# Low parts of the keys beside zeros: score products over 128 rows instead of 64

## The chip, the cores and the metric

The kernel runs on one core of one Trainium2 chip. The metric is device time in microseconds (us) of one execution. TensorE (PE) multiplies; it needs a weight load (PEld) ahead of each matmul. VectorE (DVE), ScalarE (ACT) and GpSimd (POOL) work on what comes out, and SyncE (SP) issues the DMAs of the weights.

## The reference, cut to what matters

A network of four layers over 512 tokens of 1024 channels. The parts that the change touches are the scores of two kinds of attention. In the fourth macaron layer, "stick breaking":

```
z = jnp.einsum("bqhd,bkhd->bhqk", qb, kb).astype(jnp.float32) * scale     # 16 heads of 64 channels
log_1m = jnp.where(mask, jax.nn.log_sigmoid(-z), 0.0)
between = lax.cumsum(log_1m, axis=3, reverse=True) - log_1m
att = jnp.where(mask, jnp.exp(jax.nn.log_sigmoid(z) + between), 0.0)
```

In each of the two hybrid layers after it, an attention of 8 heads over 2 groups of keys, with three branches: compressed keys (32 blocks), selected keys and windowed keys. With 512 tokens the last two branches are plain causal softmax attention over all earlier tokens. The scores of all three are products of q and k over 64 channels.

## The kernel before, in words

Everything is kept as [channels, tokens]: 128 channels on the partitions, 512 tokens along a row. To keep float32's accuracy with matmuls in the type fp32r, each operand is split into a high part (rounded to fp32r) and a low part (the rest). A dense product is then three matmuls: high by high, high by low, low by high (`three`, L274).

For the scores the heads have only 64 channels, so the three products fit into two matmuls. `query` (L1008) puts the high part of a head's q above (or below) its low part in one tile of 128 rows. `key` (L1020) makes a tile for each of the two heads of a pair in which the head's high part stands twice, above and below, and a third tile `low` with the low parts of both heads, one in each half. In `stick` (L1124) the first product runs over all 128 rows: q's high and low part against k's high part. The second multiplies k's low part by q's high part, and since these stand in one half of the partitions only (`hs`), it runs over 64 rows. The third matmul of each group adds the mask: a bf16 identity against a bf16 table with -1e30. A head has four such groups, for key tiles 0 to 3, with 512, 384, 256 and 128 queries.

The hybrid layers do the same with `doubled` (L1654), which makes the tiles of high parts and of low parts for both groups of heads, and `products` (L1648), a first matmul over 128 rows and a second over 64. `scores` (L1671) calls it for each of 4 heads of a group and adds a mask; the query tile i is the stationary operand and (i + 1) * 128 keys move. `blocks` (L1721) calls it for the 32 compressed keys, without a mask.

So there are 64 groups in `mixer1` (16 heads by 4), and in each hybrid layer 64 with a mask (8 steps by 2 groups by 4 heads) and 32 of the compressed keys: 192 with a mask, a quarter of them of each width, and 64 without.

In `mixer1` (L1002) the work of the heads overlaps. While the scores of a head are made, DVE and ACT turn those of the head before into weights, and the projections of later heads (`more`, L1075) fill in on TensorE. The last two heads have no such filler. In `nsa` (L1662) eight steps go through the same pattern: scores of one group, values of the step before, scores of the other group; `cnt` (L1765) says how far gating and retention go on at each point. A scheduler orders the instructions of each engine from this. Each engine then runs its own in that order, and waits on semaphores.

Tiles of 128x512 come from one pool of `A_BUFS` buffers (L24); PSUM has 8.

```
self.mm(z[i], k[h][:, at], q[h][:, i * P:], i != 3, False, True)          # L1135
self.mm(z[i], k[2][hs, at], q[h][hs, i * P:], False, False, True)         # L1136
self.mm(z[i][:, :P], self.masks[:, :P], self.masks[:, P:2 * P], False, True, True)
```

Of the kernel before, what the change touches and what calls it, by code (L numbers as in the profile page):

```python
# [15 lines left out]
P = 128  # L16
# [7 lines left out]
A_BUFS = 70  # L24
# [31 lines left out]
def rwkv_tables():  # L56
    """Masks for one chunk of 64 tokens, the same on both halves of the partitions: strict, identity, a level's block
    with odd rows and even columns (l = 1, .., 32), the first one transposed, the scan's restart; then the causal
    mask of two chunks side by side."""
# [44 lines left out]
class Net:  # L104
# [56 lines left out]
    def load_consts(self):  # L161
        self.consts = self.pool.tile([P, CONST.shape[1]], F32, name="consts")
        self.nc.sync.dma_start(self.consts, self.t["consts"])
        # masks that the tensor engine adds to scores: identity, and -1e30 where a key isn't before its query
        # [keys, queries] or comes after it [queries, keys]
# [51 lines left out]
    def weave(self, *gens):  # L217
        """The steps of several generators, each given with their number, in proportion."""
        todo = [[0.0, i, 1.0 / n, x] for i, (x, n) in enumerate(gens)]
        while todo:  # L220
            at = min(todo)
            at[0] += at[2]
            if next(at[3], self) is self:
                todo.remove(at)

# [1 line left out]
    def wsplit(self, w, k0, nk, segs, rows=None, pairs=False):  # L227
        """Columns segs of rows of k tiles k0.. of w, as high and low parts."""
# [15 lines left out]
        if pairs:  # L244
            # columns (g, r, d) come to stand as (r, g, d)
# [16 lines left out]
    def chunks(self, w, segs, kt, kc=4, rows=None, pairs=False, start=0):  # L262
        """For one chunk of k tiles after another: indices and (high, low) parts, 128 columns each."""
# [15 lines left out]
    def gemm(self, w, segs, rhs, kc=4, begun=None, **kw):  # L279
        """[columns, tokens], one PSUM tile for 128 columns of each of segs; begun: what begin() returned."""  # L280
# [8 lines left out]
    def begin(self, w, segs, rhs, out, kc=4, **kw):  # L289
        """The first len(rhs) of gemm's k tiles, in steps."""  # L290
# [8 lines left out]
    def by_halves(self, w, segs, rhs, **kw):  # L299
        """The same, but for one half of the tokens after the other, each in PSUM tiles of its own."""  # L300
# [9 lines left out]
    def opening(self, start, rhs):  # L310
        """A layer's first products: loads its weights, then goes over the first and the second half of the tokens."""
# [13 lines left out]
    def gemm_tok(self, w, segs, rhs):  # L325
        """[tokens of j, columns segs of w], one PSUM tile for each j."""
# [20 lines left out]
    def tok_pair(self, ws, rhs, jj):  # L347
        """[tokens of 2 jj and of 2 jj + 1, 256 columns], side by side; pauses half way."""
# [13 lines left out]
    def column_tile(self, w, c0, rhs, every=4):  # L362
        """[128 columns, tokens]; pauses after so many k tiles."""
# [8 lines left out]
    def token_sums(self, accs, ps):  # L372
        """Means over the channels, tokens on partitions: one column of PSUM for 128 tokens of each."""
# [19 lines left out]
    def spread(self, r, ps):  # L393
        """[128, n] with tokens on partitions -> PSUM [128, 128 n], the same on all partitions."""
# [80 lines left out]
    def postnorm(self, w, rhs, gname, feed, start, rows=None, begun=()):  # L475
        """x + rmsnorm(w^T rhs), and the next layer's operands and first products."""
# [47 lines left out]
    def hidden(self, w, rhs, psl, evacuate, between=None):  # L524
        """A layer's pairs of gate and up tiles; those of one step are taken up after the next step's products."""
# [33 lines left out]
    def head_rsqrt(self, sqs, ones, value, op):  # L559
        """The power -1/2 of the heads' sums of sqs, on all of a head's channels: a PSUM tile for each."""  # L560
# [26 lines left out]
    def mixer0(self, rhs, psl, feed, start):  # L587
# [16 lines left out]
        # halves for sigmoid(x) = tanh(x / 2) / 2 + 1 / 2  # L604
# [15 lines left out]
        def shift(n, ps):  # L620
            """Column tile n of the projection, mixed with its predecessor in time."""
# [17 lines left out]
        # the products of these four come before the statistics of x  # L639
# [25 lines left out]
        def quadrants(ps, lhs, rhs_):  # L665
            """A product for each chunk of each head."""
            for n in range(8):
                for rows in both:
                    self.mm(ps[rows, n * 64:n * 64 + 64], lhs(rows, n), rhs_(rows, n))
# [9 lines left out]
        def prepare(p):  # L679
            """Operands of two heads, [(head, channel), tokens]."""  # L680
# [36 lines left out]
        def pair(p):  # L717
            """Two heads up to the scan; [(chunk's parity, token), (head, chunk / 2, 64)]."""
# [23 lines left out]
            # what isn't on the way to the inverse goes on beside it  # L742
# [73 lines left out]
        def scan(p):  # L816
            """Two heads over the chunks."""
# [35 lines left out]
        def norm(p):  # L853
            """The normalisation of what a scan gave, and the gate."""
# [45 lines left out]
        # streams side by side, each with the weight of its steps  # L900
# [11 lines left out]
    def rglru(self, w_in, rhs, R, yb):  # L912
# [29 lines left out]
        def recurrence(p):  # L942
# [11 lines left out]
            # y = 8 r softplus, a = exp(-y), sqrt(1 - a^2) = sqrt(tanh(y) (1 + a^2))  # L954
# [24 lines left out]
    def softplus_neg(self, lam, scale):  # L979
        """scale * log(1 + exp(-lam)) on [128, 4], to float32's accuracy."""  # L980
# [21 lines left out]
    def mixer1(self, rhs, psl, feed, start):  # L1002
# [5 lines left out]
        def query(ps, scale):  # L1008
            """High and low parts of each head's channels above each other."""
# [10 lines left out]
        def key(ps):  # L1020
            """High parts of each head's channels, twice; low parts."""
# [3 lines left out]
            a, b, low = self.A(F32R), self.A(F32R), self.A(F32R)  # L1025
            nc.scalar.copy(a, o)
            self.tt(low, o, a.bitcast(F32), SUB)
# [3 lines left out]
            return a, b, low  # L1031
# [8 lines left out]
        def products(b, jj):  # L1040
            """Values of four heads, two token tiles side by side."""
# [82 lines left out]
    def stick(self, q, k, h, masks):  # L1124
        """One head's weights; columns of the scores of key tile i: queries from tile i on."""
# [4 lines left out]
        hs = slice(h * 64, h * 64 + 64)  # L1130
# [771 lines left out]
```

## Time and profile before

| | |
|---|---|
| median of 3 runs | 3677.62 us (3674.2 to 3680.09) |
| span of the profiled execution | 3671.4 us |
| TensorE busy | 98% of the span, 20664 matmuls |
| weight loads | 80% |
| VectorE / ScalarE / GpSimd busy | 58% / 37% / 3% |
| mean granted TensorE clock | 0.979 |

The profiled execution has its own time, and the page and all rows are of it: its span is 6.2 us below the median of the runs. TensorE counts as busy while a matmul is recorded as under way, which includes time in which it waits for its weights. So a busy share of 98% does not mean that nothing can be saved there; the distance from the start of one matmul to the start of the next tells more. In a timeline a row "x2" holds two matmuls that follow each other, under the shape of the first.

### The profile page before, as it was taken

To read this page: it belongs to the slowest core of one execution; us is meant where nothing else is said; L and a number is where in the kernel's file an instruction comes from. 1 tells how busy PE (TensorE), PEld (TensorE's weight loads), DVE (VectorE), ACT (ScalarE), POOL (GpSimd) and SP (SyncE) were. 2 spreads that over 40 slices of the span, in tenths; PEclk is the share of its full clock that TensorE was granted. 3 is DMA by queue.
4 is the path that set the end of the run, shared out by engine and by line. 5 is a ranking of instruction groups with operands and counts; after the bars stand their busy time and mean duration, and the time that the engine had idled before them with its cause. 6 is when DMAs were issued, how large, how long until landed. Compare 5 with 4: busy or idle time off the path is not lost.

```text
span 3671.4 us, 50427 instructions
## 1 busy us (share of the span) xinstructions
PE 3603.1 (98%) x20664; PEld 2926.5 (80%) x20664; DVE 2113.8 (58%) x3463; ACT 1357.6 (37%) x2220; POOL 125.8 (3%) x156
## 2 busy tenths in 40 slices
PE   8999999999999999999999999999999999999998
PEld 7888777788888888977888888657888886588887
DVE  5442777565436764576576646546654465466645
ACT  3332433133223222376432224433543354344432
POOL 0000001000000000000000001001000020010000
PEclk9999999999999999999999999989999999899999
DMA  4222310022324554311166533101323331013321
GB/s 139 94 94 89 98 42 18 26 87 95 96 88 134 192 189 135 95 52 52 58 196 189 171 114 82 41 18 46 102 94 97 112 90 35 12 47 109 98 92 63
DMA packets 359896, 337.85 MB, mean 92 GB/s; under 512 B 20214, under 2 KB 341040, under 8 KB 359664
## 3 DMA queue, kind: packets, MB, share of 16 engines
q1 hardware_dynamic: 358624, 332.46, 29.2%
q8 instruction: 162, 2.65, 0.3%
q0 software_dynamic: 1040, 2.16, 0.2%
q14 instruction: 70, 0.57, 0.1%
HBM read 332.48 MB, written 2.10 MB: 91 GB/s over the span
## 4 chain that ended last, share of the span: by engine, by line
PE 94%; DVE 3%; issue 1%; ACT 1%; POOL 1%; DMA 1%; SPq 0%; POOLq 0%; DVEq 0%; ACTq 0%
PE p L152 92%; DVE a L140 1%; PE p L1714 1%; DMA wr<-in_l_ffn_w_in 0%; POOL s L384 0%; ACT a L137 0%; DVE a L143 0%; PE p L1195 0%; ACT wh L252 0%; PE p L583 0%; DVE wl L140 0%; PE p L660 0%; DMA a<-in_x 0%; ACT a L1716 0%; POOL a L1305 0%
## 5 line engine op out<-in xcount | busy, mean ns | idle before, releaser
L152 PE MATMUL p<-a,wh 128*128 128x512 f32 (+1 forms) x8920 | 2538.9, 370 | 16.4 <-ACT a L137 6.9
L152 PEld LDWEIGHTS p<-a,wh 128*128 128x128 f32 x8920 | 1613.4, 190 | 315.0 <-issue 23.6
L152 PE MATMUL p<-a,wl 128*128 128x512 f32 (+1 forms) x4460 | 1634.3, 367 | 0.0
L140 DVE TENSOR_TENSOR wl<-wr,wh 128x1024 fp32r<-128x1024 f32 (+2 forms) x561 | 639.4, 1142 | 792.4 <-ACT wh L252 784.9
L152 PEld LDWEIGHTS p<-a,wl 128*128 128x128 f32 x4460 | 845.9, 190 | 138.7 <-issue 3.4
L252 ACT CAST wh<-wr 128x1024 fp32r<-128x1024 f32 (+2 forms) x545 | 541.5, 995 | 1060.4 <-PE p L152 1002.4
L152 PE MATMUL p<-a,a 64*64 64x64 f32 (+10 forms) x4360 | 486.4, 285 | 9.6 <-ACT a L1716 3.4
L140 DVE TENSOR_TENSOR a<-a,a 128x512 f32<-128x512 f32 (+6 forms) x752 | 443.7, 604 | 88.6 <-ACT a L156 59.0
L152 PEld LDWEIGHTS p<-a,a 64*64 64x64 f32 (+3 forms) x4360 | 300.3, 150 | 142.9 <-issue 81.6
L137 ACT ACTIVATE a<-a 128x512 f32<-128x512 f32 (+1 forms) x356 | 199.0, 590 | 350.1 <-DVE a L140 230.3
L140 DVE TENSOR_TENSOR a<-p,a 128x512 f32<-128x512 f32 (+5 forms) x334 | 203.6, 622 | 102.5 <-PE p L152 85.9
L156 ACT CAST a<-a 128x512 fp32r<-128x512 f32 x148 | 91.3, 619 | 265.5 <-DVE a L140 263.6
L143 DVE SCALAR_TENSOR_TENSOR acc<-wr,s,acc 128x1024 f32<-128x1024 f32 x84 | 107.7, 1283 | 79.6 <-DMA wr<-in_w_ada 79.2
L143 DVE SCALAR_TENSOR_TENSOR a<-p,cols,a 128x511 f32<-128x511 f32 (+1 forms) x176 | 125.5, 744 | 47.8 <-ACT a L137 46.3
L140 DVE TENSOR_TENSOR a<-a,p 128x256 f32<-128x256 f32 (+1 forms) x280 | 122.7, 466 | 36.0 <-PE p L152 34.7
L152 PE MATMUL p<-wh,a 128*128 128x256 f32 (+1 forms) x640 | 125.3, 292 | 0.1
L137 ACT ACTIVATE a<-a,cols 128x256 fp32r<-128x256 f32 (+3 forms) x156 | 83.3, 554 | 65.8 <-DVE a L140 65.8
L152 PEld LDWEIGHTS p<-wh,a 128*128 128x128 f32 x640 | 103.9, 195 | 4.6 <-issue 4.0
L137 ACT ACTIVATE a<-p 128x512 f32<-128x512 f32 (+2 forms) x144 | 75.7, 548 | 82.0 <-PE p L152 76.9
L152 PE MATMUL p<-wl,a 128*128 128x256 f32 (+1 forms) x320 | 92.8, 290 | 0.0
L137 ACT ACTIVATE a<-p,cols 128x512 f32<-128x512 f32 x92 | 68.8, 771 | 63.2 <-PE p L152 63.1
L1688 DVE TENSOR_REDUCE s<-p 128x1 f32<-128x512 f32 (+3 forms) x88 | 54.8, 638 | 60.1 <-PE p L152 59.7
(186 smaller groups left out, 1667.5 us busy)
## 6 DMA issues: line engine op xcount, KB each, us to landing
wr<-in_l_ffn_w_in SPq DMA_DIRECT2D x176, 512.0 KB
wr<-in_w_ada SPq DMA_DIRECT2D x96, 512.0 KB
wr<-in_w_up SPq DMA_DIRECT2D x88, 512.0 KB
wr<-in_l_ffn_w_out SPq DMA_DIRECT2D x68, 512.0 KB
wr<-in_w_in SPq DMA_DIRECT2D x40, 512.0 KB
wr<-in_w_down SPq DMA_DIRECT2D x34, 512.0 KB
wr<-in_l_w_qkv SPq DMA_DIRECT2D x24, 512.0 KB
wr<-in_l_w_in SPq DMA_DIRECT2D x22, 512.0 KB
```

The lines of the kernel that those rows point to most:

```text
L137: self.nc.scalar.activation(out, in_, func, bias=bias, scale=scale)
L140: self.nc.vector.tensor_tensor(out, a, b, op=op)
L143: self.nc.vector.scalar_tensor_tensor(out, a, s, b, op0=op0, op1=op1)
L152: self.nc.tensor.matmul(out, lhsT, rhs, start=start, stop=stop, skip_group_check=skip)
L156: self.nc.scalar.copy(hi, src)
L252: self.nc.scalar.copy(hi[:, :m], raw[:, :m])
L1688: nc.vector.tensor_reduce(nm[:, r0:r0 + per], ps[:, :per * n].rearrange("p (r n) -> p r n", r=per), axis=X, op=MAX, negate=True)
L1714: nc.tensor.transpose(ps[:, q4[r]], probs[g][r][:, q4[kt]], self.const("ident"))
```

## The change

The low parts of k get a tile for each head (or group) instead of one for both. In each such tile the head's low part stands in its half, and the other half is set to zero by GpSimd. The second product then runs over all 128 rows of the tile of q: the half that holds q's low part meets zeros. Its result is the same. Where VectorE took the low parts of a pair in one instruction of 128x512 in `key`, it now takes them in two of 64x512. The pool has one buffer more. Comments and docstrings were taken out as well, and are left out here.

```
-A_BUFS = 70
+A_BUFS = 71
 ...
         def key(ps):
             o = self.A()
             self.tt(o, ps, R, MUL)
             yield
-            a, b, low = self.A(F32R), self.A(F32R), self.A(F32R)
+            a, b, l0, l1 = (self.A(F32R) for _ in range(4))
+            nc.gpsimd.memset(l0[lower].bitcast(F32), 0.0)
+            nc.gpsimd.memset(l1[upper].bitcast(F32), 0.0)
             nc.scalar.copy(a, o)
-            self.tt(low, o, a.bitcast(F32), SUB)
+            self.tt(l0[upper], o[upper], a.bitcast(F32)[upper], SUB)
+            self.tt(l1[lower], o[lower], a.bitcast(F32)[lower], SUB)
             nc.scalar.copy(b[lower], a[lower])
             nc.vector.tensor_copy(b[upper], a[lower])
             nc.scalar.copy(a[lower], a[upper])
-            return a, b, low
+            return a, b, l0, l1
 ...
     def stick(self, q, k, h, masks):
-        hs = slice(h * 64, h * 64 + 64)
 ...
-            self.mm(z[i], k[2][hs, at], q[h][hs, i * P:], False, False, True)
+            self.mm(z[i], k[2 + h][:, at], q[h][:, i * P:], False, False, True)
 ...
     def products(self, out, q, kk, g, at, keys, start, stop):
-        gs = slice(g * 64, g * 64 + 64)
         self.mm(out, q[:, at], kk[g][:, keys], start, False, True)
-        self.mm(out, q[gs, at], kk[2][gs, keys], False, stop, True)
+        self.mm(out, q[:, at], kk[2 + g][:, keys], False, stop, True)

-    def doubled(self, ps, first, second, low):
+    def doubled(self, ps, *parts):
         halves = [slice(0, 64), slice(64, 128)]
-        for g, hi in enumerate((first, second)):
+        for g in range(2):
+            hi, low = parts[g], parts[2 + g]
+            self.nc.gpsimd.memset(low[halves[1 - g]].bitcast(F32), 0.0)
             for half in (halves[g], halves[1 - g]):
                 self.nc.scalar.copy(hi[half], ps[halves[g]])
             self.tt(low[halves[g]], ps[halves[g]], hi.bitcast(F32)[halves[g]], SUB)
```

In `hybrid` the tiles that go to `doubled` become four instead of three (`kc`, L1352; `keys`, L1382).

Around the scores the order on TensorE stays as it was: the same matmuls follow each other, and the second of a group reads other rows. What moves stands on VectorE and GpSimd. On VectorE, in `key` of the third pair of heads: the low parts (a_13032 before; a_13040 and a_13041 after) between those of the query and the copy of the high part.

```order
L140 TENSOR_TENSOR a_13025<-a_12939,a_13025 64x512
L140 TENSOR_TENSOR a_13024<-a_12939,a_13024 64x512
L140 TENSOR_TENSOR a_13032<-a_12972,a_13030 128x512
L1029 COPY a_13031<-a_13030 64x512
L1143 TENSOR_SCALAR a_13083<-p_13039 128x512
```

After:

```order
L140 TENSOR_TENSOR a_13033<-a_12947,a_13033 64x512
L140 TENSOR_TENSOR a_13032<-a_12947,a_13032 64x512
L140 TENSOR_TENSOR a_13040<-a_12980,a_13038 64x512
L140 TENSOR_TENSOR a_13041<-a_12980,a_13038 64x512
L1032 COPY a_13039<-a_13038 64x512
L1145 TENSOR_SCALAR a_13095<-p_13051 128x512
```

One subtraction has become two, ahead of the copy and of the next head's first step.

On GpSimd, in the first hybrid layer, from the zeros for the compressed values (a_18953 before, a_18988 after) on; the AFFINE_SELECT and what follows it belong to the gating part.

```order
L1635 MEMSET a_18953 128x512
L1444 AFFINE_SELECT a_19054<-a_19054 128x512
L1460 TENSOR_TENSOR s_19059<-s_19058,consts 128x4
L1460 TENSOR_TENSOR s_19245<-s_19244,consts 128x4
L1460 TENSOR_TENSOR s_19272<-s_19271,consts 128x4
```

After:

```order
L1606 TENSOR_TENSOR a_18624<-a_18598,cols_405 128x512
L1660 MEMSET a_18756 64x512
L1660 MEMSET a_18757 64x512
L1637 MEMSET a_18988 128x512
L1660 MEMSET a_18602 64x32 x2
L1660 MEMSET a_19079 64x512
L1660 MEMSET a_19080 64x512
L1446 AFFINE_SELECT a_19094<-a_19094 128x512
L1462 TENSOR_TENSOR s_19099<-s_19098,consts 128x4
```

All the new zeros of this layer stand ahead of the AFFINE_SELECT, which is the first instruction there to wait for long. In `mixer1`, where GpSimd had nothing to do, 16 such instructions stand one after the other.

## Rows read from the trace of the kernel before

**Rows 1.** The page: engines; the chain that ended last, by engine.

```profile
PE 3603.1 (98%) x20664; PEld 2926.5 (80%) x20664; DVE 2113.8 (58%) x3463; ACT 1357.6 (37%) x2220; POOL 125.8 (3%) x156
...
PE 94%; DVE 3%; issue 1%; ACT 1%; POOL 1%; DMA 1%; SPq 0%; POOLq 0%; DVEq 0%; ACTq 0%
```

**Rows 2.** Busy time of engines in the mixer, then both hybrid layers' attention; columns first.

```profile
core 0: us, PE busy (x) PEld busy (x) DVE busy (x) ACT busy (x) POOL busy (x), PEclk, DMA share, GB/s
1565.00:1765.00 200.00, 197.89 (x1073) 150.14 (x1071) 144.19 (x267) 133.67 (x266) 0.00 (x0) 0.97 0.15 45
2265.00:2490.00 225.00, 221.70 (x1122) 146.53 (x1120) 116.55 (x270) 91.88 (x238) 7.79 (x6) 0.91 0.12 34
3005.00:3220.00 215.00, 211.29 (x1064) 139.48 (x1063) 114.44 (x270) 87.13 (x230) 7.85 (x6) 0.91 0.11 30
```

**Rows 3.** Timeline of TensorE, a dense stream and two heads' scores: start, length, instructions.

```profile
1566.67 0.62 PE L152 MATMUL p<-a,wh 128*128 128x512 f32 x2
...
1567.35 0.62 PE L152 MATMUL p<-a,wh 128*128 128x512 f32 x2
...
1569.38 0.56 PE L152 MATMUL p<-a,a 128*128 128x128 f32 x2
...
1569.91 0.68 PE L152 MATMUL p<-a,a 128*128 128x256 f32 x2
...
1570.55 0.91 PE L152 MATMUL p<-a,a 128*128 128x512 f32 x2
...
1571.43 0.79 PE L152 MATMUL p<-a,a 128*128 128x384 f32 x2
...
1572.19 0.56 PE L152 MATMUL p<-a,a 128*128 128x128 f32 x2
...
1574.21 0.23 PE L152 MATMUL p<-masks 128*128 128x128 bf16 x1
1574.25 0.70 PE L152 MATMUL p<-a,wh 128*128 128x512 f32 x2
1574.79 0.40 PE L152 MATMUL p<-a,wl 128*128 128x512 f32 x1
```

**Rows 4.** Timeline of the weight loads, the group of 512 queries above.

```profile
1570.52 0.20 PEld L152 LDWEIGHTS p<-a,a 128*128 128x128 f32 x1
1570.96 0.18 PEld L152 LDWEIGHTS p<-a,a 64*128 64x128 f32 x1 [0.24 <-issue]
1571.39 0.10 PEld L152 LDWEIGHTS <-masks 128*128 128x128 bf16 x1 [0.25 <-issue]
```

**Rows 5.** Timeline of TensorE: matmuls of 256 columns; transposes of 128 columns.

```profile
1593.52 0.40 PE L152 MATMUL p<-wh,a 128*128 128x256 f32 x2
...
1593.88 0.40 PE L152 MATMUL p<-wh,a 128*128 128x256 f32 x2
...
2384.72 1.03 PE L1714 MATMUL p<-consts,a 128*128 128x128 f32 x8
```

**Rows 6.** Timeline of TensorE: one run of the compressed keys; a slow group of 384.

```profile
2340.05 3.47 PE L152 MATMUL p<-a,a 128*128 128x32 f32 x16
2343.45 0.58 PE L152 MATMUL p<-wh,a 128*128 128x256 f32 x1
...
2404.10 1.28 PE L152 MATMUL p<-a,a 128*128 128x384 f32 x2
```

**Rows 7.** What TensorE waited for in the mixer, then in the first hybrid layer.

```profile
PE p L152 <- ACT a L1030: 1.8, 1, 1.8
...
PE p L152 <- ACT a L1716: 1.7, 4, 1.0
```

**Rows 8.** Timelines of VectorE (last `key`) and of GpSimd (first hybrid layer).

```profile
1740.83 0.69 DVE L140 TENSOR_TENSOR a<-a,a 128x512 fp32r<-128x512 f32 x1
...
2213.27 0.52 POOL L1635 MEMSET a<- 128x512 f32 x1
2284.07 0.64 POOL L1444 TENSOR_SCALAR_AFFINE_SELECT a<-a 128x512 f32<-128x512 f32 x1 [70.28 <-ACT a L1442]
```

More of the change, by code (lines that the diff above doesn't have):

```diff
@@ L1351, in hybrid @@
         kcs = self.A(F32R)
-        kc = [kcs[:, i * 32:i * 32 + 32] for i in range(3)]
+        kc = [kcs[:, i * 32:i * 32 + 32] for i in range(4)]
         nc.gpsimd.dma_start(w2[0:64, 0:64], t["c_w2_k"][l])
@@ L1381, in keys @@
                 pass
-            kk.append([self.A(F32R) for _ in range(3)])
+            kk.append([self.A(F32R) for _ in range(4)])
             self.doubled(ps, *kk[-1])
```

## The prediction

> **What bounds the kernel now.** I read the page first: TensorE is busy for 98% of the span and makes up 94% of the chain that ended last [rows 1]. So a saving on TensorE counts, and one elsewhere counts only where TensorE waits for it. Then I asked for busy times in the three stretches in which the changed matmuls stand, the second mixer and the attention of the two hybrid layers [rows 2]. There too TensorE is busy for 198 of 200, 222 of 225 and 211 of 215 us, with VectorE at 72%, 52% and 53% and ScalarE at 67%, 41% and 41%. The two weight columns tell more: the loads take 150 of 200, 147 of 225 and 139 of 215 us there, against 80% of the whole span. TensorE is "busy" in these stretches partly with something that is neither streaming columns nor loading weights early. The granted clock is lower there as well, 0.97, 0.91 and 0.91, where it is 0.979 on average over the kernel.
>
> The timeline shows what that is. In the dense stream three matmuls of 512 columns take 0.68 us from start to start, 0.227 each, each with its own weight load under the one before [rows 3]. A group of scores with 512 queries has two such matmuls and a mask of 128 columns, and takes 0.88 (from 1570.55 to 1571.43); the other widths take 0.76 for 384, 0.64 for 256 and 0.53 for 128 [rows 3]. The weight loads say why: those of the 64-row product (1570.96) and of the mask after it (1571.39) start only when the matmul before has run out, after the load engine was idle for 0.24 and 0.25 us, though nothing that the profile shows held it ("issue"). The load of the next 128-row product starts at once behind the mask (1570.52, before the matmul at 1570.55) [rows 4]. So a step from 128 rows to 64 or back costs an unhidden load and the run-out of the matmul before; between two operations of 128 rows, even of different types, neither is seen.
>
> The Trainium skill has both sides of this. "TensorEngine Tiling (Array Packing)", section Key Properties, states that changing the tiling mode, not just the tile, drains TensorE; by that rule the second product brings two drains into each group and the change removes them, which rows 4 bear out with 0.24 and 0.25 us of idle loads. "TensorE: Matmul & The Clock Gate", Part 3, The mechanism, states that a weight load overlaps with a running matmul only when the row groups differ; by that rule two products of 128 rows would not overlap either, and the change would bring nothing. The dense stream of rows 3 speaks against it here, with 0.227 us for a matmul with a load of its own; it stands below as a rival.
>
> **The change part by part.** *The 192 groups with a mask.* After the change all three operations run over 128 rows. For the products I take stream prices: 0.227 for 512 [rows 3]; 0.120 for 256, from three in 0.36 [rows 5]; midway, 0.174, for 384. For 128 columns the load sets the pace: eight transposes take 1.03 us with the run-out of the last [rows 5], so under 0.129 each, and I take 0.115. The mask, and the load behind it that has only the short mask to hide under, I price where a dense stream follows: mask and two products of 512 from 1574.21 to 1574.79, 0.58, less 2 x 0.227, is 0.13 [rows 3]. New group: 0.58, 0.48, 0.37 and 0.36. Saved: 0.30, 0.28, 0.27 and 0.17, together 1.02 us for one of each width. With 48 of each width that is 49 us.
>
> *The load of the mask behind a 128-row product* is not in this trace, since every mask now follows a 64-row product. From below it costs nothing more than the 0.13 above; from above it stays unhidden as now, about 0.10 us (the mask's load, 0.10, in rows 4), 192 times: 19 us. I take the lower end, because the load behind the mask crosses the same change of type and is early [rows 4].
>
> *The 64 groups of compressed keys.* Sixteen products of 32 columns, eight pairs, take 3.40 us (2340.05 to 2343.45) [rows 6]: 0.425 a pair. At 0.115 each a pair takes 0.23; saved 0.195, times 64 is 12.5 us. Gross: 61 us, about 17 in the mixer and 22 in each hybrid layer.
>
> *The clock.* 0.03 of 200, 0.09 of 225 and 0.09 of 215 us, doubled since the low level is 0.5 (1.2 GHz, against 2.4), make some 91 us at the low level in the three stretches [rows 2]. A group of 384 that took 0.79 with its run-out at the high level takes 1.28 at the low one [rows 3, 6]: 38% of it is the clock, so 91 us hold up to 35 us to be won. The clock fell at 2343.1, right at the end of the run of compressed keys of rows 6, in which TensorE streams few columns. That run shrinks from 3.4 to 1.8 us, but transposes and short matmuls of the values stay beside it. Bounds: 0 (it falls as often as before; it could also fall more, below) and 35 us. I take 14, somewhat under half.
>
> *What is added.* VectorE: eight more subtractions in `key`. The one of 128 rows takes 0.69 us [rows 8]; one of 64 rows has the same columns, so I take 0.69, bounds 0.35 and 0.69: 5.5 us, hidden in the 28% of the mixer in which VectorE is idle, but for one place. In the last `key` TensorE already waits 1.8 us for the last copy L1030 [rows 7], which comes behind that subtraction: 0.7 us more. GpSimd: 16 zero fills of 64x512 in the mixer, 8 more and 4 of 64x32 in the hybrid layers. One of 128x512 takes 0.52 [rows 8]; GpSimd is idle in the mixer and 97% idle in the others [rows 2]. In the hybrid layers the new ones stand behind the fill at 2213.27 and ahead of an instruction that waited 70 us, until 2284.07 [rows 8], so there is room for some 2.6 us of fills. Cost nothing; if that cover were gone, at most 0.5 for each pair. No DMA is added, and SP's queue keeps its order. The buffer more takes no time.
>
> *What is late next.* When scores finish earlier, what depends on them or fills in beside them is needed earlier. In the mixer the 1.8 us of rows 7 are almost all of TensorE's waiting, in a hybrid layer 1.7 us at four places. Each of the 16 steps of the hybrid layers begins with four groups that get 0.7 to 1.2 us shorter, and the values behind them need weights that ACT and DVE make meanwhile. I take half a microsecond lost at each step: 8 us; bounds 0 and half of the gross saving, 30.
>
> Sum: 61 + 14 - 0.7 - 8 = 66 us. The profiled execution would go from 3671.4 to 3605; it stands 6.2 us below the median of the runs, and I carry that over: 3677.6 - 66 = 3612 us.
>
> **The rivals.**
> 1. The clock comes back nearly whole. For it: the fall right behind the run of compressed keys, and denser streams after the change. Against: short matmuls and transposes remain in the same places. 61 + 32 - 7 = 86 us, 3592.
> 2. The mask's load stays unhidden. For it: today it always is [rows 4]. Against: the change of rows explains that, and the way out of the mask is early. 66 - 19 = 47 us, 3631.
> 3. ACT and DVE become the bound: with 72% and 67% of the mixer they have little room once it is a tenth shorter, and the last heads have no filler. Half the gross saving is lost and the clock gains nothing: 61 - 31 = 30 us, 3648. Against: TensorE hardly waits in these stretches now [rows 7].
> 4. Nothing is saved, since full-height products with the same row groups don't overlap their loads either: 3678. Against: the stream of rows 3.
> 5. Slower: TensorE gets ahead of its operands in the attention of the hybrid layers, and in the gaps the clock falls. The gross 61 us stand against it; at 38% of a low-clock stretch lost [rows 3, 6], it decides from 160 us more at the low level than the 91 of now. With 190 more, 0.38 x 190 = 72 us are lost, net 11: 3689. For it: the clock is already lowest there. Against: TensorE would have to be slow for over half of the stretches, where today it idles 1.7 us for ACT in one of them.
>
> **How the numbers follow.** Chances: forecast 0.50, rival 1 0.20, rival 2 0.12, rival 3 0.12, rival 4 0.03, rival 5 0.03. The likeliest is 3612. The range goes from 3582, rival 1 with the whole 35 us and no step lost (61 + 35 = 96), to 3645, almost rival 3; what is outside is half of rival 3, rivals 4 and 5, and the edges. A difference under 0.2%, 7.4 us, can't be told from none here: faster by more than that 0.94, within it 0.03, slower 0.03.
>
> **What the profile after would show.** Right: no weight load of 64 rows in the scores; the load of the second product and that of the mask start just behind the start of the matmul before, and a group with 512 queries takes about 0.58 us, one with 128 about 0.36, a run of 16 products of 32 columns about 1.8. The mixer's stretch shrinks by some 17 us and each hybrid layer's by 20 to 30, with PEclk there above 0.91. Wrong: groups at 0.68 with an idle gap only ahead of the mask (rival 2), unchanged groups (rival 4), short groups with idle time of TensorE behind them that ends at ACT or DVE (rival 3), or a lower PEclk in the two hybrid stretches (rival 5). A wait for POOL in front of a product of scores would show that I hid the fills too easily.

## The result and the profile after

The changed kernel takes 3587.02 us (median of 4 runs, 3585.56 to 3588.3), beside 3675.91 us for the kernel before (4 runs, 3668.94 to 3680.09). The ratio is 0.9758, 95% interval 0.9744 to 0.9772: 89 us saved. The forecast was 66 us and 3612 us, with a range from 3582 to 3645; the nearest case is rival 1, the clock that comes back nearly whole, at 3592.

The page of the changed kernel, engines and the chain that ended last. TensorE has as many instructions as in [rows 1] and is as "busy" in share, but for 97 us less.

```profile
PE 3505.7 (98%) x20664; PEld 2884.3 (80%) x20664; DVE 2117.7 (59%) x3471; ACT 1358.2 (38%) x2220; POOL 139.3 (4%) x184
...
PE 91%; DVE 4%; issue 2%; ACT 1%; POOL 1%; DMA 1%; SPq 0%; POOLq 0%; DVEq 0%; ACTq 0%
```

The same three stretches as in [rows 2], now cut exactly at the matmuls that begin and end them in the kernel before (columns as there):

```profile
1564.50:1749.40 184.90, 177.41 (x1072) 144.31 (x1071) 148.47 (x274) 134.21 (x266) 5.21 (x10) 0.99 0.16 49
2250.40:2440.10 189.70, 184.45 (x1122) 128.60 (x1121) 115.31 (x270) 91.41 (x239) 7.86 (x6) 0.99 0.14 40
2954.40:3135.00 180.60, 175.04 (x1063) 121.65 (x1061) 113.48 (x270) 86.53 (x230) 7.86 (x6) 1.00 0.13 36
```

Between the same matmuls the mixer's stretch is 15.1 us shorter and those of the hybrid layers 35.4 and 34.2: 84.7 of the 87.5 us by which the span shrank (3671.4 to 3583.9). The granted clock, 0.97, 0.91 and 0.91 before, is 0.99, 0.99 and 1.00. Where each group of scores got shorter the timeline of TensorE shows (start, length, instructions, and in brackets a wait and what ended it). Read the distance from one start to the next.

```profile
1569.14 0.71 PE L152 MATMUL p<-a,a 128*128 128x512 f32 x2
1569.70 0.23 PE L152 MATMUL p<-masks 128*128 128x128 bf16 x1
1569.73 0.60 PE L152 MATMUL p<-a,a 128*128 128x384 f32 x2
...
1570.21 0.42 PE L152 MATMUL p<-a,a 128*128 128x128 f32 x2
...
1570.51 0.48 PE L152 MATMUL p<-a,a 128*128 128x256 f32 x2
...
1570.87 0.71 PE L152 MATMUL p<-a,a 128*128 128x512 f32 x2
...
1573.83 0.73 PE L152 MATMUL p<-a,wh 128*128 128x512 f32 x2 [2.17 <-DVE a L143]
```

A group of 512 queries takes 0.59 us (1569.14 to 1569.73), 384 takes 0.48, 128 takes 0.30, 256 takes 0.36; in [rows 3] they took 0.88, 0.76, 0.53 and 0.64. The weight loads beside them, in which the new thing is the row "x2" (both products now have 128 rows, and the second load follows the first without a gap):

```profile
1569.11 0.31 PEld L152 LDWEIGHTS p<-a,a 128*128 128x128 f32 x2
1569.69 0.10 PEld L152 LDWEIGHTS <-masks 128*128 128x128 bf16 x1 [0.27 <-issue]
1569.70 0.31 PEld L152 LDWEIGHTS p<-a,a 128*128 128x128 f32 x2
```

The two fp32r loads take 0.31 together and are over at 1569.42, while the first product is still under way. Of the two late loads of [rows 4] one is gone. The mask's load is still late (0.27 us idle, 0.25 before), so half of the prediction's sign for rival 2 is there, and the change of rows can't be the whole reason for that idle time. But it costs almost nothing: the next load starts 0.01 later, and the group already takes no more than the forecast gave it.

The run of compressed keys and the 384-query groups of the first hybrid layer, to be held against [rows 6]:

```profile
2318.80 1.86 PE L152 MATMUL p<-a,a 128*128 128x32 f32 x16
2320.50 0.37 PE L152 MATMUL p<-wh,a 128*128 128x256 f32 x1
...
2366.57 3.99 PE L152 MATMUL p<-a,a 128*128 128x32 f32 x22
...
2370.44 0.60 PE L152 MATMUL p<-a,a 128*128 128x384 f32 x2
2370.88 0.23 PE L152 MATMUL p<-masks 128*128 128x128 bf16 x1
2370.92 0.60 PE L152 MATMUL p<-a,a 128*128 128x384 f32 x2
```

Sixteen products take 1.70 us (2318.80 to 2320.50) instead of 3.40, 0.21 a pair (median of all 64 pairs 0.223). The row "x22" is a mixed one: 4 and 12 products of 32 columns, between them 4 of the values with 512 columns, and 2 of the first group of 384. A group of 384 behind such a run takes 0.48 from start to start; before it took 1.26 there, at the low clock (the 1.28 of [rows 6] is its length with the run-out).

What TensorE waited for, in the mixer and then in the first hybrid layer (us in total, times, longest):

```profile
PE p L152 <- ACT a L1033: 2.5, 1, 2.5
PE p L152 <- DVE a L143: 2.2, 1, 2.2
PE p L152 <- ACT a L1157: 1.4, 1, 1.4
...
PE p L152 <- ACT a L1719: 1.7, 4, 1.0
PE p L1717 <- ACT a L137: 1.5, 4, 1.0
```

L1033 is the last copy of `key`, L1030 in [rows 7]: 1.8 us there, 2.5 now. The wait of 2.2 us for DVE at the mixer's start is new, and that for L1157 was 0.2 (as L1155). In the hybrid layers the old 1.7 (L1716) stands as L1719, and the wait for ACT L137 grew from 0.2 to 1.5.

### The profile page after: what moved, and what is told of

Its sections match the earlier page's. It is cut to its first block, busy times and chain, and to the rows that moved or that the text cites. A ratio compares the mean times of both kernels' runs of the same rounds, so it can differ in the third digit from the quotient of the medians.

```text
span 3583.9 us, 50496 instructions
## 1 busy us (share of the span) xinstructions
PE 3505.7 (98%) x20664; PEld 2884.3 (80%) x20664; DVE 2117.7 (59%) x3471; ACT 1358.2 (38%) x2220; POOL 139.3 (4%) x184
## 4 chain that ended last, share of the span: by engine, by line
PE 91%; DVE 4%; issue 2%; ACT 1%; POOL 1%; DMA 1%; SPq 0%; POOLq 0%; DVEq 0%; ACTq 0%
PE p L152 90%; DVE a L140 2%; PE p L1717 1%; ACT a L137 1%; DVE a L143 1%; DVE wl L140 0%; POOL s L384 0%; ACT wh L252 0%; PE p L1197 0%; DMA wr<-in_l_ffn_w_in 0%; DMA a<-in_x 0%; PE p L660 0%; PE p L583 0%; DVE a L149 0%; ACT a L1719 0%
## 5 line engine op out<-in xcount | busy, mean ns | idle before, releaser
L140 DVE TENSOR_TENSOR a<-a,a 128x512 f32<-128x512 f32 (+8 forms) x760 | 449.9, 606 | 89.6 <-ACT a L156 59.0
L152 PE MATMUL p<-a,a 64*64 64x64 f32 (+9 forms) x4360 | 408.4, 275 | 14.5 <-ACT a L1719 3.4
L152 PEld LDWEIGHTS p<-a,a 64*64 64x64 f32 (+3 forms) x4360 | 269.9, 149 | 108.1 <-issue 49.2
L137 ACT ACTIVATE a<-a 128x512 f32<-128x512 f32 (+1 forms) x356 | 199.4, 591 | 343.5 <-DVE a L140 224.4
L143 DVE SCALAR_TENSOR_TENSOR acc<-wr,s,acc 128x1024 f32<-128x1024 f32 x84 | 107.8, 1283 | 84.2 <-DMA wr<-in_w_ada 84.1
L143 DVE SCALAR_TENSOR_TENSOR a<-p,cols,a 128x511 f32<-128x511 f32 (+1 forms) x176 | 125.6, 745 | 47.7 <-ACT a L137 46.2
L137 ACT ACTIVATE a<-a,cols 128x256 fp32r<-128x256 f32 (+3 forms) x156 | 83.6, 557 | 64.7 <-DVE a L140 64.7
L137 ACT ACTIVATE a<-p 128x512 f32<-128x512 f32 (+2 forms) x144 | 75.2, 548 | 75.7 <-PE p L152 70.9
L137 ACT ACTIVATE a<-p,cols 128x512 f32<-128x512 f32 x92 | 68.8, 772 | 63.1 <-PE p L152 63.0
L384 POOL TENSOR_TENSOR s<-s,consts 128x2 f32<-128x2 f32 (+1 forms) x18 | 14.5, 805 | 1674.1 <-DVE s L147 1651.5
```

The costliest lines, as they stand in the source:

```text
L137: self.nc.scalar.activation(out, in_, func, bias=bias, scale=scale)
L140: self.nc.vector.tensor_tensor(out, a, b, op=op)
L143: self.nc.vector.scalar_tensor_tensor(out, a, s, b, op0=op0, op1=op1)
L152: self.nc.tensor.matmul(out, lhsT, rhs, start=start, stop=stop, skip_group_check=skip)
L384: self.nc.gpsimd.tensor_tensor(r, v, self.const("mhalf")[:, :v.shape[1]], op=ALU.pow)
```

## The experiments

Each kernel is the changed one with the edit shown, but for one that starts from the kernel before. Times are compared with the kernel before, run beside them on the same chip.

**1. Rows of the second product back to 64, all else as changed.**

```
-            self.mm(z[i], k[2 + h][:, at], q[h][:, i * P:], False, False, True)
+            self.mm(z[i], k[2 + h][hs, at], q[h][hs, i * P:], False, False, True)
 ...
-        self.mm(out, q[:, at], kk[2 + g][:, keys], False, stop, True)
+        self.mm(out, q[gs, at], kk[2 + g][gs, keys], False, stop, True)
```

(`hs` and `gs` are the half with the head's or group's rows, as in the kernel before.)

> The changed kernel with both second products back on 64 rows (stick and the hybrid layers), while the tiles for each head, their zeros, the eight further subtractions and the 71st buffer stay. Theory 'fills cost nothing': 3674 to 3680 us, ratio to before 0.998 to 1.003, row groups as long as before (0.88 us for 512 queries). Rival 'the new tiles or the other placement of buffers are part of the gain or of a hidden loss': outside of that by more than 0.3%.

Measured: 3672.5 us, ratio 0.9997 [0.9986, 1.0007]. Tiles, fills, subtractions and the extra buffer cost nothing that can be measured over the whole kernel, and the whole gain comes from the rows of the product. By stages it is less even: between the same matmuls the mixer is 4.7 us longer than before and the second hybrid layer 6.5 shorter. The granted clock goes the same way: 0.95 in both, where it was 0.97 and 0.91 before. But the mixer has also 2.5 us of wait for L1033 and 1.6 for L1158 (L1157 in the changed kernel), with groups as long as before. So these two waits come from what was added on the other engines and not from the shorter groups.

**2 and 3. The mixer alone, the hybrid layers alone.** Only the second, then only the first half of the edit above.

> The changed kernel with the hybrid layers' second products back on 64 rows, so that only the 64 groups of the second mixer run over 128 rows. Theory 'unhidden loads at each change of row count': 17 us of groups and about 5 us of clock (the 13.7 us at the low level around 1750 go) less 2 to 5 us of waits: 3655 to 3662. Rival 'the gain is the clock's in the hybrid layers': 3670 or more.

> The changed kernel with stick's second products back on 64 rows, so that only the hybrid layers' 192 groups run over 128 rows. Theory: 44 us of groups and 20 to 28 us of clock less some 9 us of waits: 3605 to 3622, and with the mixer alone the two gains add up to that of the whole change (about 89 us) within 6 us. Rival 'the stages are linked, the mixer's clock carries over': the two don't add up.

Measured: 3652.0 us, ratio 0.9943 [0.9929, 0.9956], for the mixer; 3606.87, ratio 0.9817 [0.9805, 0.983], for the hybrid layers. In ratios 0.57% and 1.83% make 2.40%, against 2.42% for the whole change: the parts add up. The mixer's time is 3 us under the range that was expected for it.

**4. Before, with the products of 64 rows put together.** If what is saved is the step from 128 rows to 64 and back, it can also be saved without zeros: a head's (or step's) four second products stand one behind another.

```
             self.mm(z[i], k[h][:, at], q[h][:, i * P:], i != 3, False, True)
-            self.mm(z[i], k[2][hs, at], q[h][hs, i * P:], False, False, True)
-            self.mm(z[i][:, :P], self.masks[:, :P], self.masks[:, P:2 * P], False, True, True)
+            self.mm(z[i][:, :P], self.masks[:, :P], self.masks[:, P:2 * P], False, False, True)
+        for i in (1, 3, 2, 0):
+            at = slice(i * P, (i + 1) * P)
+            self.mm(z[i], k[2][hs, at], q[h][hs, i * P:], False, True, True)
```

(and the same in `scores` and `blocks`)

> The kernel before, all second products still over 64 rows from the shared tile, but those of a head (or of a group in a score step, or of a group of compressed keys) follow each other behind the 128-row products and masks. So a head or step has 2 changes of row count instead of 8. Theory A 'the cost sits at the change of row count': three quarters of the 61 us of groups and much of the clock go: 46 + 15 to 20 less waits, 3610 to 3628; 64-row loads within a run are early and the four products of 512, 384, 256 and 128 take about 0.65 us from start to start of the first to the last. Rival B 'a product over 64 rows is slow in itself, its load is never hidden': no gain, 3670 to 3685, since each of the four still shows an idle load engine ahead of it.

Measured: 3609.48 us, ratio 0.9824 [0.9811, 0.9836]: 64 us of the 89, just more than theory A's range allows, with every second product still on 64 rows. Its weight loads, then its timeline of TensorE ("x5" holds the four products of 64 rows, 384, 128, 256 and 512 columns, and the first of the next head):

```profile
1571.82 0.10 PEld L152 LDWEIGHTS <-masks 128*128 128x128 bf16 x1
1571.98 0.58 PEld L152 LDWEIGHTS p<-a,a 64*128 64x128 f32 x4
1572.82 0.19 PEld L152 LDWEIGHTS p<-a,a 128*128 128x128 f32 x1 [0.25 <-issue]
```

```profile
1571.99 1.27 PE L152 MATMUL p<-a,a 64*128 64x384 f32 x5
1573.11 0.23 PE L152 MATMUL p<-masks 128*128 128x128 bf16 x1
```

Four loads of 64 rows take 0.58 us together, without a gap, beside products that run; only the load that follows them, of 128 rows again, waits 0.25. So a product of 64 rows is not slow, a change of rows is. The step back to 128 rows agrees with what "TensorEngine Tiling (Array Packing)", section Key Properties, in the Trainium skill says: changing the mode, not the tile, drains TensorE. There are no zeros in this kernel, and its granted clock in the three stretches is 0.97, 0.98 and 0.96, so most of the clock's return doesn't depend on zeros. The rule of the Trainium skill in "TensorE: Matmul & The Clock Gate", Part 3, The mechanism, that a load overlaps a running matmul only where the row groups differ, is not borne out: here four loads into the same half follow each other, and in the changed kernel both products use all rows.

**5 and 6. Which part holds the clock.** One kernel has only the compressed keys on 128 rows, the other everything except the compressed keys:

```
-    def products(self, out, q, kk, g, at, keys, start, stop):
+    def products(self, out, q, kk, g, at, keys, start, stop, rows=None):
-        self.mm(out, q[:, at], kk[2 + g][:, keys], False, stop, True)
+        rs = rows or slice(0, P)
+        self.mm(out, q[rs, at], kk[2 + g][rs, keys], False, stop, True)
```

with `group[g]` as `rows` in `scores` (and `stick` on 64 rows) for the one, in `blocks` for the other.

> The changed kernel with all second products back on 64 rows, in the second mixer and in the hybrid layers' steps, but for the 64 groups of compressed keys, which run over 128 rows. Direct gain: 64 x 0.20 us = 13 us. Theory 'each run of compressed keys brings the clock down behind it': the low-level time in the hybrid layers falls from some 60 us to under 25, worth up to 15 us more: 3645 to 3655. Rival 'the clock falls for what stands around the runs': 13 us and no more, 3659 to 3663, with the low stretches where they were.

> The changed kernel with only the 64 groups of compressed keys back on 64 rows. Direct loss against the changed kernel's 3587: 13 us, 3600. Theory 'each run of compressed keys brings the clock down behind it': low-level time of 40 us or more comes back in the hybrid layers, 3608 to 3618, and PEclk there falls to about 0.93. Rival 'the clock falls for what stands around the runs': 3598 to 3602, with low-level time in the hybrid layers under 20 us as in the changed kernel.

Measured: compressed keys alone 3653.54, ratio 0.9945 [0.9927, 0.9964]; all but them 3621.61, ratio 0.9867 [0.9849, 0.9885]. The second is 34 us slower than the changed kernel's 3587, or 37 to 40 by the ratios, which allow for the other chip; the 64 pairs themselves take 64 x (0.424 - 0.223) = 13 us more. Its two hybrid stretches, then one piece of the first (columns as in [rows 2]), and TensorE's timeline there:

```profile
2254.40:2461.40 207.00, 202.42 (x1122) 141.21 (x1121) 115.69 (x270) 91.21 (x240) 7.85 (x6) 0.92 0.13 36
2975.20:3172.40 197.20, 191.98 (x1063) 133.85 (x1062) 114.00 (x271) 86.33 (x230) 7.85 (x6) 0.93 0.11 33
...
2378.00:2391.50 13.50, 12.83 (x44) 7.36 (x44) 6.85 (x25) 4.63 (x14) 0.00 (x0) 0.50 0.00 0
```

```profile
2374.45 6.12 PE L152 MATMUL p<-a,a 128*128 128x32 f32 x22
...
2380.45 0.99 PE L152 MATMUL p<-a,a 128*128 128x384 f32 x2
2381.24 0.33 PE L152 MATMUL p<-masks 128*128 128x128 bf16 x1
2381.33 0.99 PE L152 MATMUL p<-a,a 128*128 128x384 f32 x2
```

At 2378.0, among the same 22 matmuls that take 3.99 us in the changed kernel (2366.57), the clock falls to 0.50 (1.2 GHz, the low level), and the groups of 384 behind it, on 128 rows, take 0.88 us (2380.45 to 2381.33) instead of 0.48. In the kernel before a fall stands at that run too (the run is at 2395.8 to 2402.8 there); in the changed kernel there is none. The stretch of that fall before, then the 10 us behind the run in the changed kernel:

```profile
2394.30:2414.80 20.50, 19.82 (x65) 11.96 (x65) 8.46 (x28) 5.63 (x20) 0.00 (x0) 0.50 0.00 0
...
2370.00:2380.00 10.00, 9.32 (x52) 5.53 (x51) 6.79 (x24) 5.18 (x14) 0.00 (x0) 1.00 0.00 0
```

The two layers have eight such runs of compressed keys. In the profile of the kernel before a fall to 0.50 begins inside or less than 4 us beside all eight, in the kernel with only the compressed keys back on 64 rows at seven, with only them on 128 rows at two, and in the changed kernel at none. So the compressed keys do bring falls. They are not all of it: the kernel that changes nothing but them has the clock at 0.98 in the first hybrid stretch, as expected, but at 0.93 in the second, where its longest fall (17 us, from 3181.5) begins over 9 us from the nearest run:

```profile
2272.50:2480.40 207.90, 203.56 (x1121) 134.10 (x1120) 116.28 (x270) 91.98 (x239) 7.85 (x6) 0.98 0.13 36
2997.20:3202.90 205.70, 201.82 (x1063) 132.19 (x1063) 114.46 (x270) 86.90 (x230) 7.86 (x6) 0.93 0.11 31
```

Both parts together bring it back nearly whole. My theory, that the compressed keys alone decide, holds for one layer and fails for the other, each read from one profiled execution.

**7. The changed kernel again,** without an edit.

> The changed kernel as it is, so that the next ones stand beside it on one chip: 3585 to 3590 us, ratio to before 0.974 to 0.978.

Measured: 3588.02 us, ratio 0.9766 [0.9752, 0.9781].

**8 and 9. Going further.** High and low part of the compressed keys as one product of 64 columns, added on VectorE; then also the second of `key`'s subtractions on GpSimd, against the new wait for DVE L143.

```
-                    self.products(ps[:, r * 32:r * 32 + 32], q[r][g], kc, g, q4[i], slice(0, 32), True, True)
+                    self.mm(ps[:, r * 64:r * 64 + 64], q[r][g][:, q4[i]], kc[4][:, g * 64:g * 64 + 64])
 ...
-            self.tt(l1[lower], o[lower], a.bitcast(F32)[lower], SUB)
+            nc.gpsimd.tensor_tensor(l1[lower], o[lower], a.bitcast(F32)[lower], op=SUB)
```

> The changed kernel with the two products of each group of compressed keys made one: high and low parts of the keys stand side by side, 64 columns move past the same queries, and VectorE adds the two sums (16 more additions of 128x128, some 0.3 us each, beside other work). Theory 'a product of 32 columns is priced by its weight load': 64 x 0.11 = 7 us less, 3578 to 3583. Rival 'it is priced by its columns or by the additions behind it': 3585 to 3592.

> As the one with compressed keys of 64 columns, and the second of the two subtractions in key goes to GpSimd, so that VectorE has as many as before. Theory 'the subtraction added on VectorE is what made the wait of 2.2 us at the mixer's start and lengthened that for the last key from 1.8 to 2.5 us': 1 to 4 us less than the one before it, 3575 to 3581, and the wait for the last key back at 1.8 or below. Rival 'GpSimd is slower, and its order puts the next zeros behind the wait': a wait for POOL of 0.5 us or more in front of score products, and no gain.

Measured: 3585.39, ratio 0.9757 [0.9743, 0.9772], and 3582.41, ratio 0.9752 [0.9737, 0.9766]. The first theory's price was right: a group of compressed keys takes 0.112 us instead of 0.223 (medians), 7 us for all 64. The total fell by only 2.6 us, outside the range that the theory gave, and the intervals overlap; where the rest went stays open. The last time is the lowest of all, but its interval overlaps that of the changed kernel's second run (0.9752 to 0.9781) too, so it isn't shown to be better. TensorE's waits in its mixer say why so little came of it:

```profile
PE p L152 <- ACT a L1157: 3.6, 2, 2.1
PE p L152 <- ACT a L1033: 3.1, 2, 2.9
```

The 2.2 us for DVE L143 are gone, and the two for ACT grew from 3.9 to 6.7. The wait for the last key did not go back to 1.8, it grew to 2.9, so this theory failed. The subtraction takes 1.64 us on GpSimd (mean of 8), and VectorE's own, which runs beside it, takes 1.75 to 1.83 instead of 0.69.

**10 to 12. The mask's late load, and a miss.** Masks in fp32r, to rid the mask of its change of type:

```
-        self.masks = self.pool.tile([P, 3 * P], mybir.dt.bfloat16, name="masks")
-        self.nc.gpsimd.memset(self.masks, 0.0)
+        m32 = self.A()[:, :3 * P]
+        self.nc.gpsimd.memset(m32, 0.0)
 ...
+        self.masks = self.pool.tile([P, 3 * P], F32R, name="masks")
+        self.nc.vector.tensor_copy(self.masks, m32)
```

> The changed kernel with the masks in fp32r instead of bf16, so that no operation of a group changes the type. In the changed kernel the load of a bf16 mask still starts only when the product before it has streamed out (0.27 us idle after 512 columns). Theory 'that is the change of type': the mask's load starts early, and groups go to 0.565 us for 512 queries (-0.03), but to 0.32 for 128 (+0.02), since three loads of fp32r set the pace there; together within 3 us of the changed kernel, 3584 to 3590. Rival 'it is something of the mask itself': the load stays late, and as it is longer for fp32r, each group gets some 0.06 us longer: 12 us, 3595 to 3602.

Measured: 3642.63 us, ratio 0.9913 [0.9896, 0.993]. No forecast of the time held, but the theory's mechanism did. The load of a mask in fp32r starts early, 0.23 us ahead of its matmul (1599.12 and 1599.35) where a bf16 mask's starts 0.01 ahead (1569.69 and 1569.70 above):

```profile
1599.12 0.19 PEld L152 LDWEIGHTS p<-masks 128*128 128x128 f32 x1
...
1599.35 0.22 PE L152 MATMUL p<-masks 128*128 128x128 f32 x1
```

So it is the mask's type that keeps its load late, and an early load brings almost nothing: 512, 384 and 256 queries gained 0.01 to 0.02 us a group (512: 0.580 in the median, from 0.592), and 128 lost 0.04. What made the kernel slower stands far from the change: the dense stream went from 0.227 to 0.233 us for a matmul of 512 columns. The edit had moved all tiles in memory, since the first of them is now asked for ahead of the masks. Two more runs separate type from place: bf16 masks with the tiles at those places (the same edit, with `tile([P, 6 * P], mybir.dt.bfloat16)` for the masks), and the changed kernel with all tiles moved by 32 bytes (`3 * P + 16` for the masks' size).

> The masks stay in the short type, as in the changed kernel, but are first built in a 128x512 tile, and their tile is padded to the size that it has in the run with fp32r masks, so that all working tiles lie where they lay in that run: their first at byte 20256 instead of 23136 of a partition, the weight tiles' at 169312 instead of 168544. Nothing else differs from the changed kernel. Theory (what slowed the dense stream from 0.227 to 0.233 us for a matmul of 512 columns is where the tiles lie, not the masks' type): the stream takes 0.233 again, the groups take what they take in the changed kernel (0.59 for 512 queries), and the time is 3640 to 3655 us, ratio about 0.992. Rival (it is the masks' type, or something that the run with fp32r masks did otherwise): the stream takes 0.227, and the time is that of the changed kernel, 3580 to 3595 us. Anything between, with a stream of 0.229 to 0.231, would say that only a part of the placement counts.

> The changed kernel with 32 bytes of padding behind the masks and nothing else: all working and weight tiles move by 32 bytes, from byte 23136 of a partition to 23168 (the first working tile), which is a multiple of 128, as are all the others then; in the changed kernel each begins 96 bytes past a multiple of 128. Theory (what sets the pace of the dense stream is where the tiles begin against some small power of two, and in all kernels so far they stood 32 bytes past a multiple of 64, which no tile does now): the stream of 512 columns leaves 0.227 us. From a tile that begins on a multiple of 128 I would expect no more pieces to be read than from any other, so 0.213 to 0.227; at 0.220 the 10,321 matmuls would save 72 us, time 3500 to 3590 us. Rival A (what counts is a larger distance, such as how the working tiles lie against the weight tiles, which 32 bytes for both leave alone): 0.227, unchanged, 3580 to 3595 us. Rival B (the placement of the changed kernel happens to be a good one and most others are worse): 0.231 to 0.236, 3630 to 3690 us.

Measured: 3639.56, ratio 0.9917 [0.99, 0.9933], and 3587.92, ratio 0.9772 [0.9754, 0.979]. The dense stream in the first and then in the second of them:

```profile
1591.03 0.63 PE L152 MATMUL p<-a,wh 128*128 128x512 f32 x2
1591.50 0.39 PE L152 MATMUL p<-a,wl 128*128 128x512 f32 x1
1591.73 0.63 PE L152 MATMUL p<-a,wh 128*128 128x512 f32 x2
```

```profile
1566.87 0.62 PE L152 MATMUL p<-a,wh 128*128 128x512 f32 x2
1567.33 0.39 PE L152 MATMUL p<-a,wl 128*128 128x512 f32 x1
1567.55 0.62 PE L152 MATMUL p<-a,wh 128*128 128x512 f32 x2
```

Three matmuls take 0.70 us (1591.03 to 1591.73) in the one and 0.68 in the other. So it is the place and not the type, and a move of all tiles by the same 32 bytes does no harm. In the fast kernels working and weight tiles begin equally far behind a multiple of 2048 bytes (608, or 640 after the move by 32); in the slow ones 1824 and 1376 behind. The last run's theory, a small power of two, failed, and its rival A fits. That the distance between the two is what counts was not tried by itself and stays open. With places alike, fp32r masks gain nothing (3642.63 against 3639.56).

## Why the prediction was right, and where it was off

**The groups.** Priced 0.58, 0.48, 0.37 and 0.36 for 512, 384, 256 and 128; measured 0.592, 0.479, 0.362 and 0.299 (medians over the kernel, from start to start; before 0.878, 0.779, 0.646 and 0.531). Saved for one of each width 0.286 + 0.300 + 0.284 + 0.232 = 1.10 us against 1.02, times 48 is 53 against 49. Compressed keys: 64 x 0.201 = 13 against 12.5. Gross 66 instead of 61 us. The one price that was off is that of 128 columns: two products and a mask do not take three times the pace of a transpose.

**The mask's load.** The step said that it would be early; it starts as late as before. The reason given, that the load behind the mask crosses the same change of type and is early, doesn't hold the other way round: fp32r behind bf16 is early, bf16 behind fp32r is late, and fp32r behind fp32r is early (experiment 10). The price 0.13 was nevertheless right. With 512 columns the mask now starts 0.24 us behind the second product (median; 0.43 before), where a dense stream has 0.227, so its late load costs 0.01 and not the 0.10 of rival 2. What a mask does cost falls on the product behind it, which takes 0.31 to the start of the next, and that is in the row from which the price was read (1574.21 to 1574.79). So the 0.25 us of idle loads ahead of the mask, which the prediction took for a second drain, is no measure of a drain: they are still there. The distance between starts is: the step to the second product fell by 0.10 us and the step to the mask by 0.19. It is the view to look at, not the idle time of the load engine.

**The clock.** This is the mis-sized term: 14 us of up to 35. In [rows 2] some 91 us stood at the low level; after it, by the same arithmetic, it is 0.01 x 2 x 184.9 + 0.01 x 2 x 189.7 = 8. A second profile of the changed kernel (experiment 7) has as little. At 38% of the difference that is 31 us. The balance of the stretches says the same: 84.7 us saved = 66 gross - 9 more idle + clock, so the clock brought 28. The reason for taking less than half, that transposes and short matmuls of the values stay beside the compressed keys, was wrong: with them unchanged the clock hardly fell any more. The two experiments on the compressed keys show that these count for more than their own time (34 to 40 us for 13), and that they aren't the whole cause.

**Waits.** Taken: 0.7 for the last key and 8 for the steps of the hybrid layers. TensorE's time out of work in the three stretches went from 2.1, 3.3 and 3.7 us [rows 2] to 7.5, 5.2 and 5.6: 9.2 us more, close in sum by luck, wrong in place. The 0.7 came as worked out (1.8 to 2.5), and experiment 1, which has it too, shows that it comes from what was added on the other engines. But the hybrid layers lost only 2 us each, a quarter of a microsecond a step, and the mixer 5.4. At its start, which I had not looked at, VectorE's order did it. The timeline of VectorE in the changed kernel, then in the kernel before:

```profile
1569.04 2.41 DVE L140 TENSOR_TENSOR wl<-wr,wh 128x1024 fp32r<-128x1024 f32 x2
1571.48 1.39 DVE L140 TENSOR_TENSOR a<-a,a 64x512 fp32r<-64x512 f32 x2
...
1573.09 0.68 DVE L143 SCALAR_TENSOR_TENSOR a<-p,a 128x512 f32<-128x512 f32 x1
```

```profile
1568.27 1.22 DVE L140 TENSOR_TENSOR wl<-wr,wh 128x1024 fp32r<-128x1024 f32 x1
...
1569.60 0.68 DVE L143 SCALAR_TENSOR_TENSOR a<-p,a 128x512 f32<-128x512 f32 x1
1570.31 1.38 DVE L140 TENSOR_TENSOR a<-a,a 64x512 fp32r<-64x512 f32 x2
```

In the changed kernel two subtractions of weights and two of low parts stand ahead of the step that frees TensorE at 1573.83. Before, one of weights stood ahead of it, and the two of low parts behind it. Experiment 1 has the new order and no such wait, with long groups: it takes both, the new order and a TensorE that comes early. In the run with GpSimd the wait is gone, but VectorE's order there is again the one of before, so that run doesn't show what the extra subtraction does by itself.

**Stage by stage** the terms close. Mixer: 16 x 1.10 = 17.6, clock (12 - 4) x 0.38 = 3, idle -5.4: 15.2, measured 15.1. First hybrid layer: 17.6 + 32 x 0.201 = 24, clock (40.5 - 4) x 0.38 = 14, idle -2: 36, measured 35.4. Second: 24 + 38.7 x 0.38 - 1.9 = 37, measured 34.2.

**The fills** cost nothing, as said: no wait of TensorE in these stretches ends at GpSimd, whose busy time rose by 13.5 us in all. Rival 3 (ACT and DVE the bound) had its waits at the right engines, at 9 us instead of 31. Rival 4 is refuted by the groups, rival 5 by the granted clock.

## What to carry to other kernels

Among the 128-row matmuls of this kernel the products of 64 rows saved no time, and the two changes of rows around one cost 0.2 to 0.3 us: pad such an operand with zeros, or place all such matmuls together. Where the changed matmuls stand at the places at which the granted clock falls, count its return as a term of its own, up to its whole price. And an edit that changes which tile is asked for first moves every tile: time the dense stream, not only the edited place.

## What the runs showed of the hardware

- The place of tiles in memory changes the pace of a dense stream: 0.227 against 0.233 us for each matmul of 512 columns, 10,332 of them, some 60 us. Measured it is 52 to 55 us, 1.5% of this kernel.
- With that other place products of 256 columns got a little faster (median 0.117 us from start to start instead of 0.120), so no place seen here is best for both.
- A bf16 weight load behind an fp32r product starts 0.01 us ahead of its matmul, an fp32r one in the same place 0.23 ahead, and the group is hardly shorter for it (0.580 against 0.592 us).
- A subtraction of 64x512 on VectorE takes 0.69 us, and 1.75 to 1.83 beside one on GpSimd.
- The clock gave back 28 to 31 us beside 66 us of direct savings. With the compressed keys back on 64 rows it falls among their products (2378.0); in the changed kernel it stays at the high level there (1.00 in 2370.00:2380.00).
